# Padding the 64 sample tokens of a streaming encoder layer to full 128-row TensorE tiles

## The chip, the cores and the metric

The kernel runs on one core of a Trainium2 chip. The metric is the time of one execution on the device in microseconds (us); the kernel before was run three times, with a median of 824.62 us (824.10 to 824.93).

## The reference, cut to what matters

One step of a layer with two branches over the same normalised input: an mLSTM (a recurrent matrix memory, worked in chunks) and a latent attention (MLA). 512 prompt tokens start a new stream; 64 sample tokens (`DEC`) continue another one that has 128 cached keys (`PAST`) and a carried mLSTM state. The model width is 1024, with 4 mLSTM heads of 256 and 8 attention heads of 128.

```python
h = rmsnorm(x, norm_g)
(xcm, vm, i_pre, f_pre, o_pre, z_m, c_q, c_kv, k_r, z_a, g_m, g_a) = split_cols(h @ w_in)
# attention, 8 heads; a key chunk of 64 is seen by queries of the same or a later chunk
s = (einsum(qn, kn) + einsum(qr, kr)) * ATT_SCALE
s = where(k_pos // 64 <= q_pos // 64, s, -1e30);  o = softmax(s) @ v
# mLSTM, 4 heads, chunk by chunk: C, n, m are carried
s = (q @ k.T) * w_intra;  num = w_inter * (q @ C) + s @ v;  C = decay * C + (k * w_state).T @ v
y = x + (sig(g_m) * (hm * silu(z_m)) @ w_pm + sig(g_a) * (ha * silu(z_a)) @ w_pa) @ w_out
```

The same weights serve the 512 prompt tokens and the 64 sample tokens.

## The kernel before, in words

Tokens are handled in five tiles (`TILES`, line 34): four of 128 prompt tokens and one of the 64 sample tokens. Keys have six (`KTILES`, line 35): four of the prompt, one of the 128 cached ones, one of the 64 new ones. Most of the arithmetic is done as split products: a float32 operand is cut into a high and a low part (`split_of`, line 103: ScalarE copies the high part, VectorE subtracts) and three matmuls add up.

The large projections are feature-major: `fblock` (line 150) loads a block of 128 weight columns and `gemm_f` (line 121) runs 48 matmuls over all 576 tokens in two halves of 288 columns; line 126 is where all of them are issued. Here the 64 tokens are merely part of the moving columns.

Everything that works token tile by token tile meets the 64 tokens as a tile of its own:

- the first stage: `x_tile` normalises and transposes the input (line 267), `cq_tile` (line 293) and `ck_tile` with `latent` (lines 334 and 335) transpose the latent columns;
- the attention stage: `q_tile` (lines 471 and 472) and `k_tile` (line 502) transpose queries and keys for two heads at a time; `head` (line 524) forms the scores of each prompt tile (lines 529 and 531), adds the chunk mask as a matmul of a one-row operand (line 532: `indrow`, ones for the first 64 queries, times `negrow`, -1e30), and runs `soft` (line 507); the sample tokens' scores are lines 536 and 538, the transposes of their probabilities lines 552 and 553, their product with the values lines 562 and 563;
- the mLSTM stage: `v_block` transposes the values (lines 666 and 670); `mhead` (line 685) goes through the chunks in the order 4, 0, 1, 2, 3, chunk 4 being the 64 sample tokens: scores (line 745), transposed keys (line 758), three-part products through `three` (line 728, called in lines 764, 767 and 771), transposed outputs (line 789).

In each of these the slices `0:L` and `0:DEC` make the operands of the last tile 64 rows, 64 columns, or both. Line 533 is the softmax of a prompt tile:

```python
pe.matmul(ps[:, n - 64:n], indrow, negrow, start=False, stop=True)
pts.append(soft(ps[:, 0:n], P, n))
```

The order of the work: `START` and `PLAN` (lines 31 and 32) are the written order of the steps of the first two stages, and the framework's scheduler then orders each engine's instructions by their data and by a simulated timeline, so that the matmuls of one step stand between those of others. All loads and stores go through SyncE's queue. GpSimd computes the inverse square roots (`rsqrt_of`, line 73) and parts of the rotary embedding.

Of the kernel before, what the change touches and what calls it, by code (L numbers as in the profile page):

```python
# [13 lines left out]
P = 128  # L14
# [3 lines left out]
TK = SEQ + PAST + DEC  # L18
H_M, DH = 4, 256
# [8 lines left out]
# order in which the work of the first two stages is issued (see `steps` and the attention loop)  # L28
# [9 lines left out]
def layer(ctx: ExitStack, tc, A, O):  # L38
# [37 lines left out]
    negrow = const.tile([1, 64], BF16, name="negrow")  # L76
    dve.memset(negrow, NEG)
    indrow = const.tile([1, P], BF16, name="indrow")
    dve.memset(indrow, 0.0)
    dve.memset(indrow[:, 0:64], 1.0)  # L80
# [107 lines left out]
    with ExitStack() as es:  # L188
# [62 lines left out]
        def x_tile(n):  # L251
            t0, L = TILES[n]
            xt = s1.tile([P, D], F32, tag="xt", name="xt", bufs=3)
            sp.dma_start(xt[0:L], A["x_prompt"][t0:t0 + L] if n < 4 else A["x_sample"])
            if n == 0:
                sp.dma_start(nB, A["norm_g"].rearrange("o d -> (o d)").partition_broadcast(P))
            st = s1.tile([P, 8], F32, tag="st", name="st", bufs=3)
            xs = s1.tile([P, D], F32, tag="xs", name="xs", bufs=1)
            act.activation(xs[0:L], xt[0:L], AF.Square, scale=D ** -0.5, accum_out=st[0:L, 0:1])
            dve.tensor_scalar(st[0:L, 1:2], st[0:L, 0:1], EPS, None, ALU.add)  # L260
            rsqrt_of(st[0:L, 2:3], st[0:L, 1:2], L)
            dve.scalar_tensor_tensor(xs[0:L], xt[0:L], st[0:L, 2:3], nB[0:L], ALU.mult, ALU.mult)
            for q in range(2):
                ps = SA()
                for k in range(4):
                    kk = 4 * q + k
                    pe.transpose(ps[:, k * P:k * P + L], xs[0:L, kk * P:(kk + 1) * P], ident[0:L, 0:L])
                pv = ps.rearrange("p (k t) -> p k t", k=4)[:, :, 0:L]
                qk = slice(4 * q, 4 * q + 4)
                split_of(hhi[:, qk, t0:t0 + L], hlo[:, qk, t0:t0 + L], pv)  # L270
                if n == 4:
                    both(hs, qk)

        def cq_tile(n):
# [12 lines left out]
            act.activation(sq[0:L], cq, AF.Square, scale=QL ** -0.5, accum_out=s4[0:L, 0:1])  # L287
            dve.tensor_scalar(s4[0:L, 1:2], s4[0:L, 0:1], EPS, None, ALU.add)
            rsqrt_of(s4[0:L, 1:2], s4[0:L, 1:2], L)
            dve.scalar_tensor_tensor(cqn[0:L], cq, s4[0:L, 1:2], small["qn_g"][0:L], ALU.mult, ALU.mult)  # L290
            ps = SA()
            for k in range(3):
                pe.transpose(ps[:, k * P:k * P + L], cqn[0:L, k * P:(k + 1) * P], ident[0:L, 0:L])
            pv = ps.rearrange("p (k t) -> p k t", k=4)[:, 0:3, 0:L]
            split_of(cqhi[:, :, t0:t0 + L], cqlo[:, :, t0:t0 + L] if n < 4 else cqhi[:, :, T:], pv)
# [35 lines left out]
        def latent(ckn, kro, kt0, L):  # L331
            ps = SA()
            for k in range(2):
                pe.transpose(ps[:, k * P:k * P + L], ckn[0:L, k * P:(k + 1) * P], ident[0:L, 0:L])
            pe.transpose(ps[:, 2 * P:2 * P + L], kro[0:L].rearrange("p a b -> p (a b)"), ident[0:L, 0:L])
# [93 lines left out]
    with ExitStack() as es:  # L429
# [6 lines left out]
        def q_tile(wq, n, qT, qrT):  # L436
# [33 lines left out]
            for hh in range(2):  # L470
                pe.transpose(ps2[:, hh * P:hh * P + L], qs[0:L, hh, 0:NOPE], ident[0:L, 0:L])
                pe.transpose(ps2[:, (2 + hh) * P:(2 + hh) * P + L], q2[0:L, hh].rearrange("p s c -> p (s c)").bitcast(F32), ident[0:L, 0:L])  # L472
# [5 lines left out]
        def k_tile(wk, n, kT, v):  # L478
# [22 lines left out]
            for hh in range(2):  # L501
                pe.transpose(ps2[:, hh * P:hh * P + L], kn[0:L, hh], ident[0:L, 0:L])  # L502
# [4 lines left out]
        def soft(ps, L, n):  # L507
            pt = aq.tile([P, n], F32, tag=f"P{n}", name=f"P{n}", bufs=1)
# [15 lines left out]
        def head(hh, qT, qrT, kT, v, za, ha):  # L524
            pts = []
            for i in range(4):
# [9 lines left out]
            pe.matmul(ps[0:DEC, 0:nk], qT[hh][:, SEQ:T], kT[hh][:, SEQ:TK], start=True, stop=False)  # L536
            for kr in (krhi, krlo):
                pe.matmul(ps[0:DEC, 0:nk], qrT[:, hh, SEQ:T], kr[:, SEQ:TK], start=False, stop=(kr is krlo))
            pt = soft(ps[0:DEC, 0:nk], DEC, nk)
# [12 lines left out]
            pe.transpose(ps[:, 0:DEC], pt[0:DEC, 0:P], ident[0:DEC, 0:DEC])  # L552
            pe.transpose(ps[0:DEC, 64:64 + DEC], pt[0:DEC, P:nk], ident[0:DEC, 0:DEC])
            pTs = aq.tile([P, 2, DEC], F32, tag="pTs", name="pTs", bufs=1)
            act.copy(pTs[:, 0], ps[:, 0:DEC])
            act.copy(pTs[0:DEC, 1], ps[0:DEC, 64:64 + DEC])
# [5 lines left out]
            pe.matmul(ps[:, 128:128 + DEC], v[:, 4, hh], pTs[:, 0], start=True, stop=False)  # L562
            pe.matmul(ps[:, 128:128 + DEC], v[0:DEC, 5, hh], pTs[0:DEC, 1], start=False, stop=True)
            dve.tensor_tensor(za[:, SEQ:T], ps[:, 128:128 + DEC], za[:, SEQ:T], op=ALU.mult)
            split_of(ha[0][:, hh], ha[1][:, hh], za)

        def kq(p):
            qT = [aq.tile([P, T], F32, tag="qT", name="qT", bufs=4) for _ in range(2)]
            qrT = aq.tile([P, 2, T], F32R, tag="qrT", name="qrT", bufs=2)
            kT = [ak.tile([P, TK], F32, tag="kT", name="kT", bufs=4) for _ in range(2)]  # L570
            v = ak.tile([P, 6, 2, VD], F32, tag="v", name="v", bufs=2)
            wk = wload([A["w_ukv"][:, 512 * p:512 * (p + 1)]], 2, 512, cw, 6 * QH)
# [49 lines left out]
    NP = 3 + T + 3  # L622
    DV = DH + 2
    with ExitStack() as es:
# [34 lines left out]
        def v_block(b, va, e):  # L659
            ps = fblock(A["w_in"], O_V + b * P, hx)  # L660
            vf = lp.tile([P, T], F32, tag="vf", name="vf", bufs=1)
# [8 lines left out]
            pe.transpose(ps[0:DEC, 0:P], vf[:, SEQ:T], ident)  # L670
            split_of(va[0][0:DEC, 4, es_], va[1][0:DEC, 4, es_], ps[0:DEC, 0:P])
# [13 lines left out]
        def mhead(h):  # L685
# [17 lines left out]
            qf = lp.tile([P, 2, T], F32, tag="qf", name="qf", bufs=1)  # L703
            kf = lp.tile([P, 2, T], F32, tag="kf", name="kf", bufs=1)
# [7 lines left out]
            # stabilised weights of this head, keys on partitions and queries on the free axis  # L712
# [17 lines left out]
            for c in (4, 0, 1, 2, 3):  # L730
                t0, L = TILES[c]
# [36 lines left out]
                # state  # L768
# [7 lines left out]
                # normalised output  # L776
# [129 lines left out]
```

## Time and profile before

| | |
|---|---|
| median of 3 runs | 824.62 us |
| profiled execution, from first to last instruction (its span) | 822.5 us |
| TensorE matmuls busy | 810.0 us, 98% of the span, 5759 of them |
| VectorE busy | 478.7 us, 58% |
| ScalarE busy | 362.0 us, 44% |
| GpSimd busy | 141.4 us, 17% |
| TensorE clock granted | full in all 40 slices of the span (mean 0.999) |

Of the profiled execution the profile gives the span; its own time is not given beside it, and the median of the runs lies 2.1 us above the span. How to read it: PE is TensorE's matmuls, PEld its weight loads, DVE VectorE, ACT ScalarE, POOL GpSimd. The end of a matmul in the trace is modelled, so a matmul's duration overlaps that of the next one; the starts are what shows the pace. A form such as `64*128 64x64` is rows of the stationary operand * its columns, then rows x columns that stream past it.

### The profile page before, as it was taken

What the parts mean: (1) busy time and instruction counts of PE and PEld (TensorE: products, weight loads), DVE (VectorE), ACT (ScalarE), POOL (GpSimd) and SP (SyncE); (2) the same over time, 40 slices, a digit from 0 to 9 for tenths busy, and PEclk for the clock granted to TensorE, in tenths of its full rate; (3) what the DMA queues carried; (4) which work ended last, traced back from release to release, by engine and by line L of the source; (5) the groups of instructions that cost most, each with busy time, mean ns of one, the idle gap of its engine ahead of it and who ended that gap; (6) DMA issues with size and microseconds to landing.
All of it is one profiled execution on the core that took longest, in us unless ns stands there. A gap on an engine that the chain in (4) does not pass through costs nothing.

```text
span 822.5 us, 14924 instructions
## 1 busy us (share of the span) xinstructions
PE 810.0 (98%) x5759; PEld 761.5 (93%) x5759; DVE 478.7 (58%) x1211; ACT 362.0 (44%) x999; POOL 141.4 (17%) x253
## 2 busy tenths in 40 slices
PE   7899999999999999999999999999999999999998
PEld 6898997888898798889999999999999999999997
DVE  5666566755576658545534873775477355655431
ACT  5446556663555654322434544444454434332200
POOL 2343241410143133001001110110111011000000
PEclk9999999999999999999999999999999999999999
DMA  8431231013113011126223232333333432543332
GB/s 267 138 108 59 74 111 27 1 52 106 41 52 120 27 41 33 46 84 157 78 77 91 66 106 74 103 84 97 91 94 96 118 87 68 165 124 106 101 95 76
DMA packets 101742, 72.80 MB, mean 89 GB/s; under 512 B 5742, under 2 KB 95848, under 8 KB 101672
## 3 DMA queue, kind: packets, MB, share of 16 engines
q1 hardware_dynamic: 101672, 71.86, 30.5%
q8 instruction: 45, 0.74, 0.4%
q14 instruction: 25, 0.20, 0.1%
HBM read 64.24 MB, written 7.61 MB: 87 GB/s over the span
## 4 chain that ended last, share of the span: by engine, by line
PE 94%; DMA 3%; DVE 1%; ACT 1%; issue 0%; SPq 0%; POOL 0%; DVEq 0%; ACTq 0%
PE mm L126 58%; PE sk L143 10%; PE sk L852 3%; PE sa L852 3%; PE sa L529 2%; PE sa L728 2%; PE sa L559 2%; PE sk L728 2%; PE sk L136 2%; PE sa L531 1%; PE sa L547 1%; PE sk L745 1%; PE sa L136 1%; PE sk L502 1%; DMA part<-in_w_in 1%; DMA E<-gscr 1%
## 5 line engine op out<-in xcount | busy, mean ns | idle before, releaser
L105 DVE TENSOR_TENSOR wlo<-raw,whi 128x1024 fp32r<-128x1024 f32 (+1 forms) x88 | 108.5, 1234 | 92.1 <-ACT whi L104 87.1
L104 ACT CAST whi<-raw 128x1024 fp32r<-128x1024 f32 (+1 forms) x88 | 92.6, 1055 | 135.2 <-PE mm L126 91.9
L126 PE MATMUL mm<-hhi,whi 128*128 128x288 f32 x896 | 147.1, 300 | 1.1 <-ACT hhi L104 1.1
L126 PE MATMUL mm<-hhi,wlo 128*128 128x288 f32 x896 | 146.6, 299 | 0.0
L126 PE MATMUL mm<-hlo,whi 128*128 128x288 f32 x896 | 145.7, 298 | 0.0
L126 PEld LDWEIGHTS mm<-hhi,whi 128*128 128x128 f32 x896 | 126.6, 188 | 2.1 <-ACT hhi L104 1.4
L126 PEld LDWEIGHTS mm<-hlo,whi 128*128 128x128 f32 x896 | 127.1, 188 | 1.3 <-issue 0.5
L126 PEld LDWEIGHTS mm<-hhi,wlo 128*128 128x128 f32 x896 | 126.9, 188 | 1.2 <-issue 0.5
L74 POOL TENSOR_TENSOR r<-r,mhalf 128x2 f32<-128x2 f32 (+3 forms) x44 | 37.2, 844 | 165.4 <-DVE r L495 109.4
L126 PE MATMUL mm<-ha,whi 128*128 128x288 f32 x256 | 48.2, 307 | 0.6 <-DVE part L595 0.6
L126 PEld LDWEIGHTS mm<-ha,whi 128*128 128x128 f32 x256 | 37.3, 188 | 2.7 <-DVE part L595 1.1
L511 ACT ACTIVATE P<-sa,sc 128x128 f32<-128x128 f32 (+4 forms) x40 | 20.1, 503 | 36.4 <-DVE sc L510 35.6
L752 POOL TENSOR_TENSOR qi<-qf,wi 128x256 f32<-128x256 f32 (+1 forms) x16 | 11.9, 744 | 105.7 <-ACT qf L710 54.3
L595 DVE TENSOR_TENSOR part<-part,mm 128x288 f32<-128x288 f32 x48 | 21.4, 452 | 11.8 <-PE mm L126 11.6
L74 POOL TENSOR_TENSOR sc<-sc,mhalf 128x1 f32<-128x1 f32 (+1 forms) x20 | 13.0, 648 | 87.0 <-DVE sc L784 87.0
L126 PE MATMUL mm<-ha,wlo 128*128 128x288 f32 x128 | 27.5, 296 | 0.0
L105 POOL TENSOR_TENSOR qi<-qi,qi 128x256 fp32r<-128x256 f32 (+1 forms) x16 | 10.7, 668 | 85.3 <-ACT qi L104 85.3
L529 PE MATMUL sa<-kT,qT 128*128 128x128 f32 (+3 forms) x64 | 23.4, 447 | 0.0
L510 DVE TENSOR_REDUCE sc<-sa 128x1 f32<-128x128 f32 (+4 forms) x40 | 18.3, 457 | 8.5 <-PE sa L532 6.4
L728 PE MATMUL sk<-va,kw 128*128 128x258 f32 (+1 forms) x120 | 22.2, 290 | 0.1
L823 DVE SCALAR_TENSOR_TENSOR mt<-tgm,mm 128x288 f32<-128x288 f32 x16 | 7.3, 454 | 25.1 <-PE mm L126 25.1
L474 ACT ACTIVATE qT<-sk,gqn_c 128x128 f32<-128x128 f32 (+1 forms) x40 | 12.2, 354 | 18.8 <-PE sk L472 18.8
(353 smaller groups left out, 1641.0 us busy)
## 6 DMA issues: line engine op xcount, KB each, us to landing
raw<-in_w_in SPq DMA_DIRECT2D x56, 512.0 KB, 3.8
raw<-in_w_pa SPq DMA_DIRECT2D x8, 512.0 KB
raw<-in_w_pm SPq DMA_DIRECT2D x8, 512.0 KB, 4.2
raw<-in_w_uq SPq DMA_DIRECT2D x4, 576.0 KB, 4.0
gmscr<-tg SPq DMA_DIRECT2D x8, 288.0 KB
tgm<-gmscr SPq DMA_DIRECT2D x8, 288.0 KB, 4.3
xt<-in_x_prompt SPq DMA_DIRECT2D x4, 512.0 KB, 6.7
raw<-in_w_ukv SPq DMA_DIRECT2D x4, 512.0 KB, 3.8
```

Source lines behind the costliest of these rows:

```text
L74: pool.tensor_tensor(dst, ms, mhalf[0:n, 0:dst.shape[-1]], op=ALU.pow)
L104: act.copy(hi, src)
L105: (eng or dve).tensor_tensor(lo, src, hi.bitcast(F32), op=ALU.subtract)
L126: pe.matmul(ps[j], a[:, k0 + k, c0:c0 + P], b[:, k, sl], start=(n == 0), stop=(n == len(trip) - 1))
L136: pe.matmul(out, x[:, k, t0:t0 + P], a, start=(i == 0), stop=(i == len(trip) - 1))
L143: pe.matmul(out, b[:, k, t0:t0 + L], a[:, k, c0:c0 + n], start=(i == 0), stop=(i == len(trip) - 1))
L510: dve.tensor_reduce(sc[0:L, 0:1], ps, AX.X, ALU.max, negate=True)
L511: act.activation(pt[0:L, 0:n], ps, AF.Exp, bias=sc[0:L, 0:1], accum_out=sc[0:L, 1:2])
L529: pe.matmul(ps[:, 0:n], qT[hh][:, q0:q0 + P], kT[hh][:, 0:n], start=True, stop=False)
L595: dve.tensor_tensor(part[:, f, sl], part[:, f, sl], ps[j], op=ALU.add)
L728: pe.matmul(out, x, y, start=(first and i == 0), stop=(last and i == 2))
L852: pe.matmul(ps[0:L, 0:NB], x[:, 4 * u + k, t0:t0 + L], w[u][i][:, k], start=(q == 0), stop=(q == len(trip) - 1))
```

## The change

The last tile's operands become full. Transposes take all 128 rows (what lies in the rows beyond the 64 tokens is not used afterwards). Queries, keys and values of the attention and of the mLSTM get tiles 640 tokens wide (`TP`), whose last 64 columns GpSimd sets to zero; so do the last 64 rows of the values and the last 64 columns of the probabilities (`pt5`). The chunk mask is no longer a matmul: VectorE writes -1e30 into the score tile in PSUM. Two ScalarE copies of the transposed probabilities become one. The merge stage takes other buffers for its gate tiles, and a scratch area for DMA descriptors shrinks, to make room. Comments are dropped.

```diff
+TP = SEQ + P
-    negrow = const.tile([1, 64], BF16, name="negrow")
-    indrow = const.tile([1, P], BF16, name="indrow")
...
-                    pe.transpose(ps[:, k * P:k * P + L], xs[0:L, kk * P:(kk + 1) * P], ident[0:L, 0:L])
+                    pe.transpose(ps[:, k * P:(k + 1) * P], xs[:, kk * P:(kk + 1) * P], ident)
...
-                pe.transpose(ps2[:, hh * P:hh * P + L], qs[0:L, hh, 0:NOPE], ident[0:L, 0:L])
+                pe.transpose(ps2[:, hh * P:(hh + 1) * P], qs[:, hh, 0:NOPE], ident)
...
+        pt5 = aq.tile([P, 2 * P], F32, name="pt5")
+        pool.memset(pt5[:, PAST + DEC:2 * P], 0.0)
...
                 for kr in (krhi, krlo):
-                    pe.matmul(ps[:, 0:n], qrT[:, hh, q0:q0 + P], kr[:, 0:n], start=False, stop=False)
-                pe.matmul(ps[:, n - 64:n], indrow, negrow, start=False, stop=True)
+                    pe.matmul(ps[:, 0:n], qrT[:, hh, q0:q0 + P], kr[:, 0:n], start=False, stop=(kr is krlo))
+                dve.memset(ps[0:DEC, n - DEC:n], NEG)
                 pts.append(soft(ps[:, 0:n], P, n))
...
-            pe.matmul(ps[0:DEC, 0:nk], qT[hh][:, SEQ:T], kT[hh][:, SEQ:TK], start=True, stop=False)
+            pe.matmul(ps[:, 0:nk], qT[hh][:, SEQ:TP], kT[hh][:, SEQ:TK], start=True, stop=False)
...
-            pe.transpose(ps[:, 0:DEC], pt[0:DEC, 0:P], ident[0:DEC, 0:DEC])
-            pe.transpose(ps[0:DEC, 64:64 + DEC], pt[0:DEC, P:nk], ident[0:DEC, 0:DEC])
+            for j in range(2):
+                pe.transpose(ps[:, j * P:(j + 1) * P], pt5[:, j * P:(j + 1) * P], ident)
             pTs = aq.tile([P, 2, DEC], F32, tag="pTs", name="pTs", bufs=1)
-            act.copy(pTs[:, 0], ps[:, 0:DEC])
-            act.copy(pTs[0:DEC, 1], ps[0:DEC, 64:64 + DEC])
+            act.copy(pTs, ps.rearrange("p (k t) -> p k t", k=4)[:, 0:2, 0:DEC])
...
-            pe.matmul(ps[:, 128:128 + DEC], v[0:DEC, 5, hh], pTs[0:DEC, 1], start=False, stop=True)
+            pe.matmul(ps[:, 256:256 + DEC], v[:, 5, hh], pTs[:, 1], start=False, stop=True)
...
-            qT = [aq.tile([P, T], F32, tag="qT", name="qT", bufs=4) for _ in range(2)]
+            qT = [aq.tile([P, TP], F32, tag="qT", name="qT", bufs=4) for _ in range(2)]
+            for hh in range(2):
+                pool.memset(qT[hh][:, T:TP], 0.0)
+            pool.memset(qrT.bitcast(F32)[:, :, T:TP], 0.0)
+            pool.memset(v[DEC:P, 5], 0.0)
...
-            vf = lp.tile([P, T], F32, tag="vf", name="vf", bufs=1)
+            vf = lp.tile([P, TP], F32, tag="vf", name="vf", bufs=1)
+            pool.memset(vf[:, T:TP], 0.0)
...
+            pool.memset(qf[:, :, T:TP], 0.0)
+            pool.memset(kf[:, :, T:TP], 0.0)
...
             for c in (4, 0, 1, 2, 3):
-                t0, L = TILES[c]
+                t0, L = c * P, P
...
-            tg = lp.tile([P, NP], F32, tag=("xp", "th", "vf")[f % 3], name="tgm", bufs=1)[:, 0:T]
+            tg = lp.tile([P, NP if f % 3 == 0 else NP - 3], F32, tag=("xp", "th", "acc")[f % 3], name="tgm", bufs=2 if f % 3 == 2 else 1)[:, 0:T]
...
-    nc = _bacc.Bacc("TRN2", target_bir_lowering=False, num_devices=1)
+    nc = _bacc.Bacc("TRN2", target_bir_lowering=False, num_devices=1, dynamic_dma_scratch_size=1024)
```

The same edit as the first two pairs of lines is made to the transposes of lines 293, 334, 335, 472 and 502, to line 538, and to the value transposes of line 670.

## Rows read from the trace of the kernel before

**Rows 1.** The page's busy table: us, share of the span, instructions of three engines.

```profile
PE 810.0 (98%) x5759; PEld 761.5 (93%) x5759; DVE 478.7 (58%) x1211; ACT 362.0 (44%) x999; POOL 141.4 (17%) x253
```

**Rows 2.** The page's chain of work that ended last, shares of the span.

```profile
PE 94%; DMA 3%; DVE 1%; ACT 1%; issue 0%; SPq 0%; POOL 0%; DVEq 0%; ACTq 0%
```

**Rows 3.** The chain in order of time: start us, us, what; one unbroken run.

```profile
369.05 55.22 PE mm L126 x414
```

**Rows 4.** Timeline of PE around 110 us: start us, us, line, op, tiles, form, count.

```profile
110.08 0.28 PE L531 MATMUL sa<-krhi,qrT 128*128 128x256 f32 x1
110.20 0.28 PE L531 MATMUL sa<-krlo,qrT 128*128 128x256 f32 x1
110.41 0.20 PE L532 MATMUL sa<-negrow,indrow 1*128 1x64 bf16 x1
110.54 1.20 PE L126 MATMUL mm<-hhi,whi 128*128 128x288 f32 x7
111.57 0.83 PE L126 MATMUL mm<-hlo,whi 128*128 128x288 f32 x5
...
112.49 0.65 PE L126 MATMUL mm<-hlo,whi 128*128 128x288 f32 x3
112.97 0.30 PE L126 MATMUL mm<-hhi,wlo 128*128 128x288 f32 x1
```

**Rows 5.** Timeline of PE around 266 us, the query tile of the sample tokens.

```profile
265.69 0.69 PE L126 MATMUL mm<-hlo,whi 128*128 128x288 f32 x4
266.32 0.27 PE L472 MATMUL sk<-ident,q 64*128 64x64 f32 x1
266.43 0.22 PE L471 MATMUL sk<-ident,qs 64*128 64x64 f32 x1
266.49 0.22 PE L472 MATMUL sk<-ident,q 64*128 64x64 f32 x1
266.65 0.80 PE L126 MATMUL mm<-hlo,whi 128*128 128x288 f32 x4
267.29 1.22 PE L126 MATMUL mm<-hhi,wlo 128*128 128x288 f32 x8
```

**Rows 6.** Groups of PE by line and form: xcount | busy us, mean ns.

```profile
L532 PE MATMUL sa<-negrow,indrow 1*128 1x64 bf16 x32 | 6.3, 198 | 0.0
```

**Rows 7.** Timeline of PE around 145 us: the sample tokens' scores lie between these.

```profile
144.88 0.29 PE L126 MATMUL mm<-ha,whi 128*128 128x288 f32 x1
...
145.81 0.32 PE L126 MATMUL mm<-ha,whi 128*128 128x288 f32 x1
```

**Rows 8.** Timeline of PE around 356 us: lines 562 and 563.

```profile
356.23 0.33 PE L562 MATMUL sa<-pTs,v 128*128 128x64 f32 x2
...
356.85 0.40 PE L126 MATMUL mm<-hhi,whi 128*128 128x288 f32 x1
357.09 1.23 PE L126 MATMUL mm<-hlo,whi 128*128 128x288 f32 x8
```

**Rows 9.** Timeline of PE around 438 us: chunk 4's scores and transposed keys.

```profile
437.68 0.42 PE L126 MATMUL mm<-uhi,wlo 128*128 128x288 f32 x2
438.03 0.33 PE L745 MATMUL sk<-qf,kf 128*64 128x64 f32 x2
...
438.35 1.30 PE L126 MATMUL mm<-hhi,whi 128*128 128x288 f32 x8
439.48 0.30 PE L126 MATMUL mm<-hlo,whi 128*128 128x288 f32 x1
```

**Rows 10.** Timeline of PE around 446 us: the 15 products of chunk 4 lie between these.

```profile
445.28 0.29 PE L126 MATMUL mm<-hhi,whi 128*128 128x288 f32 x1
...
447.81 0.71 PE L745 MATMUL sk<-qf,kf 128*128 128x128 f32 x4
```

**Rows 11.** Groups of DVE by line and form: xcount | busy us, mean ns | idle before.

```profile
L195 DVE MEMSET ones<- 128x128 f32 x1 | 0.2, 165 | 0.1
L641 DVE MEMSET xp<- 128x3 f32 x8 | 0.5, 61 | 0.0
```

More of the change, by code (lines that the diff above doesn't have):

```diff
@@ L74, in rsqrt_of @@
         pool.tensor_tensor(dst, ms, mhalf[0:n, 0:dst.shape[-1]], op=ALU.pow)
-    negrow = const.tile([1, 64], BF16, name="negrow")
-    dve.memset(negrow, NEG)
-    indrow = const.tile([1, P], BF16, name="indrow")
-    dve.memset(indrow, 0.0)
-    dve.memset(indrow[:, 0:64], 1.0)
     cols = const.tile([P, 82], F32, name="cols")
@@ L292, in cq_tile @@
             for k in range(3):
-                pe.transpose(ps[:, k * P:k * P + L], cqn[0:L, k * P:(k + 1) * P], ident[0:L, 0:L])
+                pe.transpose(ps[:, k * P:(k + 1) * P], cqn[:, k * P:(k + 1) * P], ident)
             pv = ps.rearrange("p (k t) -> p k t", k=4)[:, 0:3, 0:L]
@@ L333, in latent @@
             for k in range(2):
-                pe.transpose(ps[:, k * P:k * P + L], ckn[0:L, k * P:(k + 1) * P], ident[0:L, 0:L])
-            pe.transpose(ps[:, 2 * P:2 * P + L], kro[0:L].rearrange("p a b -> p (a b)"), ident[0:L, 0:L])
+                pe.transpose(ps[:, k * P:(k + 1) * P], ckn[:, k * P:(k + 1) * P], ident)
+            pe.transpose(ps[:, 2 * P:3 * P], kro.rearrange("p a b -> p (a b)"), ident)
             pv = ps.rearrange("p (k t) -> p k t", k=4)[:, 0:2, 0:L]
@@ L470, in q_tile @@
             for hh in range(2):
-                pe.transpose(ps2[:, hh * P:hh * P + L], qs[0:L, hh, 0:NOPE], ident[0:L, 0:L])
-                pe.transpose(ps2[:, (2 + hh) * P:(2 + hh) * P + L], q2[0:L, hh].rearrange("p s c -> p (s c)").bitcast(F32), ident[0:L, 0:L])
+                pe.transpose(ps2[:, hh * P:(hh + 1) * P], qs[:, hh, 0:NOPE], ident)
+                pe.transpose(ps2[:, (2 + hh) * P:(3 + hh) * P], q2[:, hh].rearrange("p s c -> p (s c)").bitcast(F32), ident)
             for hh in range(2):
@@ L501, in k_tile @@
             for hh in range(2):
-                pe.transpose(ps2[:, hh * P:hh * P + L], kn[0:L, hh], ident[0:L, 0:L])
+                pe.transpose(ps2[:, hh * P:(hh + 1) * P], kn[:, hh], ident)
             for hh in range(2):
@@ L505, in k_tile, with soft @@
             yield
-        def soft(ps, L, n):
-            pt = aq.tile([P, n], F32, tag=f"P{n}", name=f"P{n}", bufs=1)
+        pt5 = aq.tile([P, 2 * P], F32, name="pt5")
+        pool.memset(pt5[:, PAST + DEC:2 * P], 0.0)
+        def soft(ps, L, n, pt=None):
+            pt = aq.tile([P, n], F32, tag=f"P{n}", name=f"P{n}", bufs=1) if pt is None else pt
             sc = ap.tile([P, 4], F32, tag="sc", name="sc", bufs=4)
@@ L535, in head @@
             nk = PAST + DEC
-            pe.matmul(ps[0:DEC, 0:nk], qT[hh][:, SEQ:T], kT[hh][:, SEQ:TK], start=True, stop=False)
+            pe.matmul(ps[:, 0:nk], qT[hh][:, SEQ:TP], kT[hh][:, SEQ:TK], start=True, stop=False)
             for kr in (krhi, krlo):
-                pe.matmul(ps[0:DEC, 0:nk], qrT[:, hh, SEQ:T], kr[:, SEQ:TK], start=False, stop=(kr is krlo))
-            pt = soft(ps[0:DEC, 0:nk], DEC, nk)
+                pe.matmul(ps[:, 0:nk], qrT[:, hh, SEQ:TP], kr[:, SEQ:TK], start=False, stop=(kr is krlo))
+            soft(ps[:, 0:nk], P, nk, pt5[:, 0:nk])
             pT = aq.tile([P, 10 * P], F32, tag="pT", name="pT", bufs=1)
@@ L561, in head @@
             dve.tensor_tensor(za[:, 0:SEQ], of, za[:, 0:SEQ], op=ALU.mult)
-            pe.matmul(ps[:, 128:128 + DEC], v[:, 4, hh], pTs[:, 0], start=True, stop=False)
-            pe.matmul(ps[:, 128:128 + DEC], v[0:DEC, 5, hh], pTs[0:DEC, 1], start=False, stop=True)
-            dve.tensor_tensor(za[:, SEQ:T], ps[:, 128:128 + DEC], za[:, SEQ:T], op=ALU.mult)
+            pe.matmul(ps[:, 256:256 + DEC], v[:, 4, hh], pTs[:, 0], start=True, stop=False)
+            pe.matmul(ps[:, 256:256 + DEC], v[:, 5, hh], pTs[:, 1], start=False, stop=True)
+            dve.tensor_tensor(za[:, SEQ:T], ps[:, 256:256 + DEC], za[:, SEQ:T], op=ALU.mult)
             split_of(ha[0][:, hh], ha[1][:, hh], za)
         def kq(p):
-            qT = [aq.tile([P, T], F32, tag="qT", name="qT", bufs=4) for _ in range(2)]
-            qrT = aq.tile([P, 2, T], F32R, tag="qrT", name="qrT", bufs=2)
+            qT = [aq.tile([P, TP], F32, tag="qT", name="qT", bufs=4) for _ in range(2)]
+            qrT = aq.tile([P, 2, TP], F32R, tag="qrT", name="qrT", bufs=2)
+            for hh in range(2):
+                pool.memset(qT[hh][:, T:TP], 0.0)
+            pool.memset(qrT.bitcast(F32)[:, :, T:TP], 0.0)
             kT = [ak.tile([P, TK], F32, tag="kT", name="kT", bufs=4) for _ in range(2)]
             v = ak.tile([P, 6, 2, VD], F32, tag="v", name="v", bufs=2)
+            pool.memset(v[DEC:P, 5], 0.0)
             wk = wload([A["w_ukv"][:, 512 * p:512 * (p + 1)]], 2, 512, cw, 6 * QH)
@@ L669, in v_block @@
             ps = SK()
-            pe.transpose(ps[0:DEC, 0:P], vf[:, SEQ:T], ident)
-            split_of(va[0][0:DEC, 4, es_], va[1][0:DEC, 4, es_], ps[0:DEC, 0:P])
+            pe.transpose(ps[:, 0:P], vf[:, SEQ:TP], ident)
+            split_of(va[0][:, 4, es_], va[1][:, 4, es_], ps[:, 0:P])
         def gate_block(b, gate, e):
@@ L702, in mhead @@
             w = wload([A["wq_m"][h], A["wk_m"][h]], 4, DH)
-            qf = lp.tile([P, 2, T], F32, tag="qf", name="qf", bufs=1)
-            kf = lp.tile([P, 2, T], F32, tag="kf", name="kf", bufs=1)
+            qf = lp.tile([P, 2, TP], F32, tag="qf", name="qf", bufs=1)
+            kf = lp.tile([P, 2, TP], F32, tag="kf", name="kf", bufs=1)
+            pool.memset(qf[:, :, T:TP], 0.0)
+            pool.memset(kf[:, :, T:TP], 0.0)
             for dst, k0, s in ((qf, 0, 0.5), (kf, 2, 0.5 / 16.0)):
@@ L789, in mhead @@
                     pe.transpose(ps[:, e * P:e * P + L], hn[0:L, e * P:(e + 1) * P], ident[0:L, 0:L])
-                dve.tensor_tensor(tm[:, :, t0:t0 + L], ps.rearrange("p (k t) -> p k t", k=4)[:, 0:2, 0:L],
-                                  gate[:, :, t0:t0 + L], op=ALU.mult)
+                n = TILES[c][1]
+                dve.tensor_tensor(tm[:, :, t0:t0 + n], ps.rearrange("p (k t) -> p k t", k=4)[:, 0:2, 0:n],
+                                  gate[:, :, t0:t0 + n], op=ALU.mult)
             for s, dst in ((0, Cp), (1, Cs)):
```

## The prediction

> **What bounds the kernel now.** I read the busy table first: TensorE's matmuls fill 98% of the span, VectorE 58%, ScalarE 44%, GpSimd 17% [rows 1]. A busy share alone proves nothing, so the chain of waits came next: 94% of the work that ended last is PE's, 3% DMA, 1% each VectorE and ScalarE [rows 2]. So the time is PE's instruction stream, and an edit is worth what it takes out of that stream. Matmul durations overlap, so I price by start times. The pace of the large projections is the yardstick: 414 matmuls in 55.22 us, or 0.1334 us each [rows 3]. Wherever the timeline shows k of them between two starts, I take k x 0.1334 off, and what is left is the price of what stands among them.
>
> **What a small operand costs.** The query tile of the sample tokens shows it [rows 5]: from 265.69 to 267.29 are 1.60 us with eight projection matmuls (1.067), so three 64-row transposes cost 0.533. Three full transposes of a prompt tile, between 111.57 and 112.97 [rows 4], cost 1.40 - 1.067 = 0.333, 0.11 each. Yet inside the small group the last two start only 0.06 apart (266.43, 266.49) [rows 5]: at 0.06 each the three would be 0.18. The other 0.35 is paid on going into the small form and coming out of it. A group of k small transposes thus loses 0.35 in the change of form, and padding adds 0.05 to each: a group of one gains 0.30, of two 0.25, of three 0.20, of eight loses 0.05.
>
> **The sum, part by part.**
>
> *The mask matmul* (line 532, 32 times [rows 6]). From 110.20 to 111.57 are 1.37 us: one L531 at 0.12 (110.08 to 110.20), seven projections (0.934), and 0.316 for the mask, almost all of it form change [rows 4]. 32 x 0.316 = 10.1 us, the largest term. The sizes other than this one (256 columns) are taken alike.
>
> *The transposes.* Query tiles: four in each of four pairs of heads; [rows 5] has three together and the fourth elsewhere, so 0.20 + 0.30, four times: 2.0. Key tiles: two each, four times, together (0.25) or apart (0.60); I take 0.42, halfway, as both occur: 1.7. Probabilities (lines 552, 553): a pair for each of eight heads: 2.0. Outputs of chunk 4 (line 789): four pairs, 1.0. First stage: a group of eight (-0.05), one of three (0.20), latents as two and one (0.25 + 0.30): 0.7. Together 7.4; were every group kept whole, 4 x 0.35 and 4 x 0.17 less, 5.3. The transposes of line 670 have 128 rows already, 64 columns only; the trace has no row that splits off their cost. I take nothing, nearest to the full transposes; the other end is eight pairs' worth less padding, 2 us.
>
> *Scores of the sample tokens* (lines 536, 538). From 144.88 to 145.81 are 0.93, less one projection, 0.80 [rows 7]. Padded, the float32 ones have 192 columns: from 0.11 for 128 [rows 4], 0.165 each, two. The other two lie between 0.06 [rows 5] and the 0.12 of a 256-column L531 [rows 4]; I take 0.09, as columns scale. That is 0.51, so 0.29 a head, 2.3 in all (0.23 to 0.35: 1.8 to 2.8).
>
> *Products with the values* (lines 562, 563). From 356.23 to 357.09, less one projection, are 0.727 [rows 8]. Four full ones cost between 4 x 0.06 and 4 x 0.11; I take the upper, because their stationary operand is that of a full transpose. 0.29 a head, 2.3 (up to 3.9).
>
> *mLSTM chunk 4.* Scores and a key transpose: 437.68 to 439.48 less ten projections is 0.466 [rows 9]; three full ones 0.33; 0.13, eight times: 1.1. The 15 products: 445.28 to 447.81 less one projection is 2.40 [rows 10]; at 258 of 288 columns a full one is 0.12, 15 are 1.80; 0.60, four times: 2.4.
>
> Sum: 10.1 + 7.4 + 2.3 + 2.3 + 1.1 + 2.4 = 25.6 us.
>
> **What is added.** 32 memsets on VectorE, each 64 x 64 in PSUM. The nearest rows are 0.061 for three columns and 0.165 for 128, both in SBUF [rows 11]; I take 0.12, 3.8 us on an engine with 42% free. On the softmax's path they replace a matmul that took 0.316, so that path does not grow even at 0.165. Their wait is not new: the row maximum behind them on VectorE already waits for the same scores. Some 33 memsets on GpSimd (four for each pair of heads, one for each value block, two for each mLSTM head, one once) zero 64 columns; its price for that is not in my rows. GpSimd is busy 17% [rows 1], so I cost them at nothing; cover gone, they hold up the inverse square roots queued behind them, which key and query tiles wait for. ScalarE loses one copy a head; VectorE, ScalarE and GpSimd work on 64 more columns in chunk 4. All of it lies beside PE's stream. SyncE's queue is untouched: no transfer is added or moved. The scratch size and the other buffers for the gate tiles are taken at nothing: neither adds an instruction to PE's stream.
>
> **What comes back.** The savings are thickest in the attention stage. PE then arrives earlier at places where it has just caught up with VectorE or GpSimd, and the scheduler may lay the stream out anew. Between nothing and half of the gain can be lost there. I take 1.0 us, near the lower end, because VectorE and ScalarE together hold 2% of the chain [rows 2].
>
> Net 24.6 us off the profiled span of 822.5: 797.9. The median of the runs is 2.1 above that span, which I keep: 800.0, equally 824.62 - 24.6.
>
> **The rivals.**
>
> *Half of it turns into waits.* Softmax and key chains set the pace where PE no longer does: 824.6 - 12.8 = 811.8. For it: VectorE rises to some 482 of 798 us. Against it: the chain of waits [rows 2], and that the chain through the mask gets shorter. Chance 0.15.
>
> *Only the padding is paid (slower).* The 0.35 could be no price of the form but of meeting an operand that another engine has just written; it would then stay behind the padded forms, and the change would add 0.05 to 62 transposes and to 16 scores of chunk 4, 3.9 us, and take away only the masks' own column time, 32 x 0.06 = 1.9: +2.0, 826.6. It decides if a padded group still costs 0.35 above its members. Against it stands the full triple [rows 4], whose operands come from the same engines and which shows no such extra. The Trainium skill, in TensorEngine Tiling (Array Packing), section Theoretical Speedup, speaks for this rival: an operand of at most 64 rows or columns is there worth up to twice the pace, so padding would give that away. The trace agrees inside a group (0.06 against 0.11), not for a group as a whole. Chance 0.06.
>
> *More than the sum.* The value products at 0.06 give 1.6 more, line 670 up to 2, the narrower masks some more, and nothing comes back: 824.6 - 25.6 - 3.9 = 795.1. Chance 0.06.
>
> *It does not do what it says.* A new order of the stream that costs as much as is saved, or forms that stay small in the built program: 824.6. Chance 0.03.
>
> **How the numbers follow.** The forecast has 0.70: 800.0, the time of the likeliest case, from about 797 to 804 by the bounds of its terms. The range 794 to 812 takes in the case above the sum and, at its edge, the half-lost one; beyond it lie the two last rivals and the far part of the half-lost one, under 2 in 10. Faster by over 0.2% (1.65 us, about what a measurement of this kernel can tell from no change) are the forecast, the half-lost and the larger gain, 0.91; within it the idle change, 0.03; slower the padding rival, 0.06.
>
> **What would show it.** PE's matmul count falls by 32, to 5727, and of the forms with 64 rows or 64 columns at the lines named none is left. L531's successors start at the ordinary pace; a query triple of the sample tokens costs 0.33 instead of 0.53; chunk 4's 15 products take about 1.8 instead of 2.4 us. The large projections stay at 0.1334 us and the clock stays full. Each is a step of the sum. The forecast is wrong if a padded group still pays 0.35 (the padding rival), or if the forms are gone, the groups are cheap and the PE timeline shows new idle time before transposes of probabilities (line 547), keys (502) or queries (471), released by VectorE or GpSimd: then the half-lost rival holds, and the sum was right but not the cover.

## The result, and the profile after

| | before | after |
|---|---|---|
| median of the runs, us | 824.36 (823.66 to 824.93, 4 runs) | 809.76 (808.73 to 810.22, 4 runs) |
| ratio to before | | 0.9816, 95% interval 0.9803 to 0.9829 |
| profiled execution: span, us | 822.5 | 808.4 |
| PE matmuls | 5759 | 5727 |

The change gains 14.6 us. The forecast was 24.6 (800.0), so its sign and its range hold, but the time lies nearer to the half-lost rival (811.8) than to the forecast. Some 10 us of the forecast gain did not come.

The busy table of the page after, and below it the chain that ended last:

```profile
PE 791.6 (98%) x5727; PEld 762.3 (94%) x5727; DVE 481.0 (60%) x1240; ACT 362.2 (45%) x991; POOL 148.2 (18%) x286
...
PE 91%; DVE 4%; DMA 3%; ACT 1%; issue 1%; SPq 0%; POOL 0%; ACTq 0%; POOLq 0%
```

PE's share is 98% again, as in [rows 1], and shows nothing of the loss. The chain does: VectorE's share goes from 1% to 4%, PE's from 94% to 91% [rows 2].

**Prices of the sum, looked up.** The timeline of PE, first where the mask was, then a query tile of the sample tokens, then chunk 4 of the mLSTM (start us, us, line, operation, tiles, form, count). Line numbers have moved: 530 was 531, 467 and 468 were 471 and 472, 733 was 728.

```profile
109.03 0.28 PE L530 MATMUL sa<-krlo,qrT 128*128 128x256 f32 x1
109.14 0.29 PE L122 MATMUL mm<-hhi,wlo 128*128 128x288 f32 x1
...
232.01 0.43 PE L122 MATMUL mm<-ha,wlo 128*128 128x288 f32 x2
232.28 0.27 PE L468 MATMUL sk<-ident,q 128*128 128x128 f32 x1
232.39 0.27 PE L467 MATMUL sk<-ident,qs 128*128 128x128 f32 x1
232.50 0.27 PE L468 MATMUL sk<-ident,q 128*128 128x128 f32 x1
232.52 0.78 PE L122 MATMUL mm<-ha,whi 128*128 128x288 f32 x4
233.14 0.42 PE L122 MATMUL mm<-ha,wlo 128*128 128x288 f32 x2
...
436.04 0.41 PE L733 MATMUL sk<-va,kw 128*128 128x258 f32 x2
...
437.86 0.61 PE L750 MATMUL sk<-qf,kf 128*128 128x128 f32 x4
```

- Behind the second L530 (109.03) the next projection starts 0.11 later, at the ordinary pace, and nothing stands between them.
- From 232.01 to 233.14 are 1.13 us with six projections (0.80): the padded triple costs 0.33, as forecast. With 64 rows it was 0.53 [rows 5].
- The 15 products of chunk 4 take 1.82 us (436.04 to 437.86), forecast 1.80; before it was 2.40 [rows 10].
- The sample tokens' products with the values take 0.39 where a head of the middle has them unhindered (lines 560 and 561, from 151.82 to 152.21), forecast 0.44; before it was 0.73 [rows 8].

**The added work.** The memset of the mask on VectorE (count | busy, mean ns | idle before):

```profile
L531 DVE MEMSET sa<- 64x64 f32 x32 | 3.5, 112 | 7.0 <-PE sa L530 6.6
```

It took 0.112 us where 0.12 was the estimate. The 33 memsets that zero columns or rows are on GpSimd. Its busy time grows by 6.8 us (141.4 to 148.2), and in the list of waits below PE never waits for it.

**Where the gain comes through and where not.** The chain in order of time has one landmark in both kernels, the unbroken run of 414 projections behind the attention stage; it stood at 369.05 [rows 3]:

```profile
360.14 55.22 PE mm L122 x414
```

Up to this run 8.9 us are gained (369.05 - 360.14). The forecast's terms for that part (masks 10.1, scores 2.3, value products 2.3, and of the transposes all but chunk 4's outputs, 6.4) add up to 21.1. Behind it 5.2 are gained (822.5 - 369.05 = 453.5, against 808.4 - 360.14 = 448.3), forecast 4.5 (1.1, 2.4 and 1.0). So the mLSTM terms were about right, and 12 us of loss lie ahead of this run, where the attention stage is. PE's waits from 100 us to that run, the wait at its start included (engine, line, waited for: us in total, times, longest), first before, then after:

```profile
PE mm L126 <- DVE part L595: 0.6, 2, 0.4
```

```profile
PE mm L122 <- ACT ha L100: 1.2, 1, 1.2
PE mm L122 <- DVE part L597: 0.8, 3, 0.4
PE sk L139 <- DVE qs L439: 0.5, 1, 0.5
PE sa L546 <- ACT pT L547: 0.5, 1, 0.5
PE sa L528 <- ACT qT L470: 0.5, 1, 0.5
PE sa L530 <- DVE qrT L471: 0.4, 1, 0.4
PE sa L546 <- ACT P L510: 0.2, 1, 0.2
PE sk L132 <- DVE qrT L471: 0.2, 1, 0.2
PE sk L498 <- DVE kn L494: 0.2, 1, 0.2
PE sk L498 <- ACT kT L500: 0.2, 1, 0.2
```

One row becomes ten, 0.6 us becomes 4.7: beside part, the running sum of the output projections, PE now waits for query tiles (qs, qT, qrT), key tiles (kn, kT), probabilities (P, pT) and the last head's output (ha). The prediction had named waits of this kind as the sign of the half-lost rival. Between 160 and 300 us the list has no wait of PE at all.

The largest sit at the last head. The timeline of its end, PE and what it waits for:

```profile
342.47 1.26 PE L546 MATMUL sa<-ident,P 128*128 128x128 f32 x7 [0.22 <-ACT P L510]
...
344.20 0.33 PE L546 MATMUL sa<-ident,P 128*128 128x128 f32 x1 [0.46 <-ACT pT L547]
...
347.06 0.39 PE L561 MATMUL sa<-pTs,v 128*128 128x64 f32 x2
347.10 0.69 DVE L559 TENSOR_TENSOR za<-sa,za 128x512 f32<-128x512 f32 x1 [2.52 <-PE sa L557]
347.70 0.21 DVE L562 TENSOR_TENSOR za<-sa,za 128x64 f32<-128x64 f32 x1
347.95 0.67 ACT L100 CAST ha<-za 128x576 fp32r<-128x576 f32 x1 [2.90 <-DVE za L562]
348.67 1.20 PE L122 MATMUL mm<-ha,whi 128*128 128x288 f32 x5 [1.22 <-ACT ha L100]
```

No projection stands among the transposes of the probabilities here, so each chain is seen at its full length: exponential, transpose, copy, transpose; and at the end value product, VectorE's two products, ScalarE's cast, next projection. In the kernel before the last head's instructions lie among the 96 projections of the gate blocks G6 and G7 (48 each) and PE is never idle, as the windows of the kernel before show (us; busy us of PE, PEld, DVE, ACT, POOL with counts; granted clock; DMA share; GB/s):

```profile
340.00:350.00 10.00, 10.00 (x70) 8.67 (x69) 5.04 (x14) 4.07 (x10) 0.70 (x2) 1.00 0.16 52
350.00:360.00 10.00, 10.00 (x66) 8.82 (x66) 3.00 (x5) 3.15 (x8) 0.00 (x0) 1.00 0.29 84
```

In the kernel after the scheduler has placed G6 and G7 ahead of the last head, though the written plan is the same, and nothing is left to put beside it. Why it did so is not shown.

The windows of the end of this stretch, after:

```profile
346.00:349.00 3.00, 1.78 (x12) 1.46 (x11) 1.17 (x3) 0.67 (x1) 0.00 (x0) 1.00 0.00 0
349.00:354.00 5.00, 4.85 (x24) 4.39 (x23) 1.74 (x5) 0.00 (x0) 0.00 (x0) 0.67 0.01 3
```

PE is busy 1.78 of 3 us, and in the 5 us behind that the granted clock is 0.67 on average, between the full level of 2.4 GHz and 1.2 GHz: some 1.65 us (0.33 x 5) in this execution.

### The profile page after: what moved, and what is told of

It reads as the page before. It is cut to its first block, busy times and chain, and to the rows that moved or that the text cites. A ratio compares the mean times of both kernels' runs of the same rounds, so it can differ in the third digit from the quotient of the medians.

```text
span 808.4 us, 14939 instructions
## 1 busy us (share of the span) xinstructions
PE 791.6 (98%) x5727; PEld 762.3 (94%) x5727; DVE 481.0 (60%) x1240; ACT 362.2 (45%) x991; POOL 148.2 (18%) x286
## 4 chain that ended last, share of the span: by engine, by line
PE 91%; DVE 4%; DMA 3%; ACT 1%; issue 1%; SPq 0%; POOL 0%; ACTq 0%; POOLq 0%
PE mm L122 58%; PE sk L139 9%; PE sa L858 3%; PE sk L858 3%; PE sa L733 2%; PE sa L557 2%; PE sk L733 2%; PE sk L132 2%; PE sa L528 2%; PE sk L750 1%; PE sa L546 1%; PE sa L132 1%; PE sa L530 1%; DMA part<-in_w_in 1%; PE sk L498 1%; DMA E<-gscr 1%
## 5 line engine op out<-in xcount | busy, mean ns | idle before, releaser
L122 PE MATMUL mm<-ha,whi 128*128 128x288 f32 x256 | 50.3, 314 | 2.0 <-ACT ha L100 1.2
L122 PEld LDWEIGHTS mm<-ha,whi 128*128 128x128 f32 x256 | 39.0, 194 | 5.4 <-DVE part L597 2.2
L75 POOL TENSOR_TENSOR sc<-sc,mhalf 128x1 f32<-128x1 f32 x20 | 12.1, 605 | 84.9 <-DVE sc L789 84.9
L101 POOL TENSOR_TENSOR qi<-qi,qi 128x256 fp32r<-128x256 f32 x16 | 11.8, 737 | 71.6 <-ACT qi L100 71.6
L510 ACT ACTIVATE P<-sa,sc 128x128 f32<-128x128 f32 (+3 forms) x32 | 16.9, 527 | 16.7 <-DVE sc L509 16.5
L733 PE MATMUL sk<-va,kw 128*128 128x258 f32 x120 | 21.5, 284 | 0.1
L122 PEld LDWEIGHTS mm<-ha,wlo 128*128 128x128 f32 x128 | 21.0, 192 | 0.0
```

Of the source, the lines that this page charges most:

```text
L75: pool.tensor_tensor(dst, ms, mhalf[0:n, 0:dst.shape[-1]], op=ALU.pow)
L101: (eng or dve).tensor_tensor(lo, src, hi.bitcast(F32), op=ALU.subtract)
L122: pe.matmul(ps[j], a[:, k0 + k, c0:c0 + P], b[:, k, sl], start=(n == 0), stop=(n == len(trip) - 1))
L510: act.activation(pt[0:L, 0:n], ps, AF.Exp, bias=sc[0:L, 0:1], accum_out=sc[0:L, 1:2])
L733: pe.matmul(out, x, y, start=(first and i == 0), stop=(last and i == 2))
```

## The experiments

Three theories stood against each other, by the names that the expectations use. **Form**: what was lost or won lies in the operands' forms themselves. **Order**, later called **fill** or **cover**: the chains of the heads, the last one's above all, are no longer beside enough projections, and the place of the plan's blocks decides. **Pace**: VectorE's and ScalarE's chains set the pace of the whole attention stage, however the projections lie. All ratios are to the kernel before, run on the same chip; its medians there were 824.36 to 825.19 us. The variants change the form or the order of the work, not its result.

| kernel | median us | ratio [95% interval] |
|---|---|---|
| mask alone | 817.96 | 0.9911 [0.9895, 0.9928] |
| mLSTM padding alone | 819.96 | 0.9936 [0.9921, 0.9950] |
| after, one-row mask matmul kept | 818.11 | 0.9915 [0.9900, 0.9930] |
| after, mask matmul with 128 rows | 812.80 | 0.9848 [0.9831, 0.9864] |
| after | 809.76 | 0.9816 [0.9803, 0.9829] |
| after, G7 held | 809.51 | 0.9810 [0.9795, 0.9825] |
| after, G6 and G7 held | 808.87 | 0.9802 [0.9787, 0.9817] |
| after, G5 late | 807.53 | 0.9793 [0.9777, 0.9810] |
| after, G5 late, G6 and G7 held | 807.94 | 0.9796 [0.9783, 0.9809] |
| after, G4 and G5 late | 808.59 | 0.9803 [0.9789, 0.9816] |
| before, G5 late | 826.29 | 1.0017 [1.0008, 1.0026] |
| before, G6 and G7 early | 828.84 | 1.0045 [1.0029, 1.0062] |

### Is it the form of the mask, or the mask?

Two kernels from the one after, each with the mask as a matmul again. In the first its operands have one row, as before. In the second the same matmul has 128 rows, 127 of them zero:

```diff
-                    pe.matmul(ps[:, 0:n], qrT[:, hh, q0:q0 + P], kr[:, 0:n], start=False, stop=(kr is krlo))
-                dve.memset(ps[0:DEC, n - DEC:n], NEG)
+                    pe.matmul(ps[:, 0:n], qrT[:, hh, q0:q0 + P], kr[:, 0:n], start=False, stop=False)
+                pe.matmul(ps[:, n - 64:n], indrow, negrow, start=False, stop=True)
...
-    negrow = const.tile([1, 64], BF16, name="negrow")
+    negrow = const.tile([P, 64], BF16, name="negrow")
+    dve.memset(negrow, 0.0)
+    dve.memset(negrow[0:1], NEG)
```

(indrow likewise.) Expected of the one-row mask:

> The changed kernel with the chunk mask put back as the one-row matmul, everything else padded. Form theory (a change of operand form costs PE about 0.16 us on the way in and again on the way out, and PE is the pace): 32 masks at 0.32 us come back, 809.8 + 10 = 820, between 816 and 821. Pace theory (other engines set the pace of the attention stage now, PE has slack there): the masks are mostly hidden, 810 to 814.

Expected of the full one:

> As the run before, but the mask's two operands are filled with zeros to 128 rows: the same 32 matmuls in the same places of PE's stream, no change of form. Form theory: each costs its own 0.03 to 0.11 us instead of 0.32, so 7 to 9 us below the run with the one-row mask, 811 to 813. If the price were that of the instruction or of its wait: the same time as the run with the one-row mask.

Measured 818.11 and 812.80, each inside the form theory's range: 5.3 us by the form of the operands alone, less than the 7 to 9 expected between the two. The same place in both timelines, the one-row mask first:

```profile
108.91 0.28 PE L535 MATMUL sa<-krlo,qrT 128*128 128x256 f32 x1
109.12 0.20 PE L536 MATMUL sa<-negrow,indrow 1*128 1x64 bf16 x1
109.25 0.33 PE L473 MATMUL sk<-ident,q 128*128 128x128 f32 x1
...
109.55 0.38 PE L127 MATMUL mm<-hhi,wlo 128*128 128x288 f32 x1
```

```profile
107.95 0.28 PE L536 MATMUL sa<-krlo,qrT 128*128 128x256 f32 x1
108.08 0.20 PE L537 MATMUL sa<-negrow,indrow 128*128 128x64 bf16 x1
108.11 0.31 PE L474 MATMUL sk<-ident,q 128*128 128x128 f32 x1
...
108.40 0.38 PE L128 MATMUL mm<-hhi,wlo 128*128 128x288 f32 x1
```

From the score matmul to the next projection, with the same three transposes between, are 0.64 us with the one-row mask and 0.45 with the full one. So the change of form costs 0.19 here, 32 times 6.1, of which 5.3 reach the end. The kernel after has no mask matmul but a projection more in this bracket (109.03 to 109.52, 0.49 - 0.133 = 0.36). So the one-row mask costs 0.28 in this place (0.32 in [rows 4]), and 0.09 of that is the matmul itself. The forecast had put "almost all of it" down to the form; the total, which is what the sum used, was right.

### Which part of the change pays?

The mask alone in the kernel before (the memset in place of the matmul, no padding), and the mLSTM stage alone padded:

```diff
-                pe.matmul(ps[:, n - 64:n], indrow, negrow, start=False, stop=True)
+                dve.memset(ps[0:DEC, n - DEC:n], NEG)
```

> The kernel before with the chunk mask alone replaced by the VectorE memset; all 64-row forms stay. Form theory: 10 us less PE stream in the attention stage, of which some turns into waits where the stage's fill runs out: 7 to 10 us faster than before, 815 to 818. Pace theory: the softmax chains take over at once, 3 to 5 us faster, 820 to 822.

```diff
-            qf = lp.tile([P, 2, T], F32, tag="qf", name="qf", bufs=1)
+            qf = lp.tile([P, 2, TP], F32, tag="qf", name="qf", bufs=1)
+            pool.memset(qf[:, :, T:TP], 0.0)
...
-                t0, L = TILES[c]
+                t0, L = c * P, P
```

> The kernel before with the mLSTM stage alone padded (value transposes, chunk 4, the merge's buffers). In that stage PE is covered by projections everywhere, so every change of form that goes is gained. Form theory: the sum of its terms, 1.1 + 2.4 + 1.0 = 4.5 us faster than before, between 4 and 5.5 (820 against 825). A theory in which half of any saving turns into waits: 2.2 us.

The mask alone gains 7.0 us of its 10.1, at the lower end of what was expected. PE's wait for the last head's ha (1.1 us) is there already with nothing padded. The mLSTM part gains 5.0, a little over its 4.5. The padding without the mask's edit gains 7.1 (the kernel with the one-row mask), and taking off the mLSTM's 5.0 leaves some 2 for all that was padded ahead of it, priced at 11.0. So most of what was priced for the padding of the attention stage was lost, and the mLSTM term was not.

### Does the last head lack its cover?

Three kernels put projections beside the last head, by an edit of the order alone. In the plan H6 and H7 are the heads of the last pair, P3 is their output projection, and G0 to G7 are the gate blocks. In the first two kernels G7, or G6 and G7, can't be issued until the third score tile of the last head is computed; in the third the plan has G5 behind the last pair's heads. The edit of the second (the first has 7 alone), and that of the third:

```diff
-                gm_block(i, aq.tile([P, T], F32, tag="tg", name="tg", bufs=1))
+                with tc.issue_after(gate_ins[0]) if i in (6, 7) else ExitStack():
+                    gm_block(i, aq.tile([P, T], F32, tag="tg", name="tg", bufs=1))
```

> The changed kernel, only the gate block G7 (48 projection matmuls) is held behind the third score tile of the last attention head, so that it again lies among that head's softmax and transposes. Order theory (the scheduler put G6 and G7 ahead of the last head, whose 5 us of waits are now bare): 3 to 5 us faster than the changed kernel, 805 to 807. Pace theory: the waits only move, 809 to 811.

> As the run before, with G6 held back as well: the last head is covered as in the kernel before, but the head before it is left without projections. Order theory: the last head gains 5 us and the head before it loses 1 to 4, 806 to 809, above the run that holds G7 alone. Pace theory: 809 to 811.

```diff
-PLAN = "... H4 G4 Z5 Z6 H5 G5 K3 Z7 P2 H6 H7 G6 G7 P3"
+PLAN = "... H4 G4 Z5 Z6 H5 K3 Z7 P2 H6 H7 G5 G6 G7 P3"
```

> The changed kernel with one token of the written order moved: gate block G5 (48 projections, 6.4 us) goes from before key block K3 to the last three fill blocks, so that both last heads have projections to lie among. Fill theory (the last heads' chains are longer than the PE work now left to cover them, 6 to 7 us of waits; the middle has work to spare): 4 to 6 us faster than the changed kernel, 804 to 806. If the stage as a whole is bound by other engines, the waits turn up in the middle instead: 808 to 811.

G7 held gave 809.51, nothing gained, as the pace theory had it and outside the order theory's 805 to 807. G6 and G7 held gave 808.87, 0.9 less than after: inside the order theory's 806 to 809, though not above the kernel that holds G7 alone, and not told from nothing, as the intervals overlap. PE's waits in the second from 310 to 333 us say why (its lines stand up to three further on than after's):

```profile
PE sa L538 <- ACT qT L470: 0.9, 1, 0.9
PE sa L555 <- DVE pt L512: 0.7, 1, 0.7
PE sa L549 <- ACT pT L550: 0.6, 1, 0.6
PE sa L531 <- DVE qrT L471: 0.4, 1, 0.4
PE sk L468 <- DVE q L463: 0.4, 1, 0.4
```

The last head is covered now, as the window of this kernel shows:

```profile
340.00:350.00 10.00, 10.00 (x69) 9.10 (x68) 3.63 (x5) 2.82 (x6) 0.00 (x0) 1.00 0.28 82
```

The head before it, from which the two blocks were taken, waits instead, 3.0 us in these rows.

G5 late gave 807.53, the lowest of all and 2.2 under after: short of the 804 to 806 expected, and under the 808 to 811 of the rival, though the intervals of the two ratios still overlap (0.9777 to 0.9810, and 0.9803 to 0.9829). Its windows show PE full where it was bare, and the wait for ha at the end still there:

```profile
340.00:346.00 6.00, 6.00 (x41) 5.21 (x40) 2.25 (x3) 2.17 (x5) 0.00 (x0) 1.00 0.16 55
346.00:349.00 3.00, 1.78 (x12) 1.41 (x12) 1.58 (x3) 0.67 (x1) 0.00 (x0) 1.00 0.59 167
349.00:354.00 5.00, 4.85 (x36) 4.62 (x35) 2.72 (x7) 0.00 (x0) 0.00 (x0) 1.00 0.02 3
```

The clock stays full behind that wait, where the kernel after had lost some 1.65 us. So much of the gain in the profiled execution is the clock's: the run of 414 starts at 357.56 in place of 360.14, 2.6 earlier, and 1.65 of that is the clock. Among the runs whose mean granted clock is 1.000, G5 late took 807.12 and 807.35 and the kernel after 808.73, which puts the order's own share at some 1.5 us. And waits turn up where G5 was taken away: from 285 to 335 us PE now waits three times for part, 1.1 us in total, where the kernel after has 0.2 (and 0.4 for qrT).

The same edit in the kernel before, as a control:

> The same move of G5 in the kernel before. Fill theory: there the last heads were covered already, so nothing is gained, within 1.5 us of before, 823.5 to 826.5. If the move helped by itself, whatever the forms, it would gain as much here as in the padded kernel, 4 us or more.

It gave 826.29, 1.3 us slower and inside the 823.5 to 826.5 expected: where the last head has its cover, the move brings nothing.

### The same loss without any padded form

The plainest test of the theory: the kernel before, all small forms and masks kept, and only the order of the plan edited so that G6 and G7 come ahead of the last pair's heads.

```diff
-PLAN = "... K3 Z7 P2 H6 H7 G6 G7 P3"
+PLAN = "... K3 Z7 P2 G6 G7 H6 H7 P3"
```

> The kernel before, small forms and mask matmuls kept, with the blocks G6 and G7 of the plan put ahead of the last pair's score pass, so that the last head's softmax, transposes and value products have no projection matmuls beside them. Cover theory (what the change lost in the attention stage is the projections that used to cover each head's chain, above all the last head's): the bare last head costs 4 to 6 us in this kernel too, 828.5 to 831 us, with new PE waits on VectorE and ScalarE in the last 20 us of the attention stage. Theory that the loss comes with the padded forms or the memset: no padded form is here, 823.5 to 826 us.

828.84, 3.7 us slower than before on the same chip (825.15) and inside the cover theory's numbers. The four runs spread: the two with a mean granted clock of 1.000 took 826.75 and 827.84, the two with 0.998 took 829.83 and 829.95. Its waits at the last head are those of the kernel after, line for line (ACT ha, ACT pT, ACT P):

```profile
PE mm L126 <- ACT ha L104: 1.1, 1, 1.1
PE sa L547 <- ACT pT L548: 0.5, 1, 0.5
PE sa L547 <- ACT P L511: 0.2, 1, 0.2
```

And so is the clock behind them (its windows):

```profile
356.00:363.00 7.00, 5.45 (x25) 3.42 (x25) 3.56 (x9) 2.02 (x7) 0.00 (x0) 1.00 0.22 65
363.00:368.00 5.00, 4.85 (x24) 4.58 (x23) 1.76 (x4) 0.00 (x0) 0.00 (x0) 0.66 0.00 0
```

The run of 414 starts at 373.69 in its chain, 4.6 us later than before [rows 3], of which 1.7 is that clock (0.34 x 5). So the bare last head alone costs some 3 us here, 1.6 and 2.7 in the two runs at the full clock.

### Can all of it be covered by the order?

Two more orders of the kernel after: G5 late together with G6 and G7 held, and G4 and G5 both moved behind a score pass.

```diff
-PLAN = "... H4 G4 Z5 Z6 H5 G5 K3 Z7 P2 H6 H7 G6 G7 P3"
+PLAN = "... H4 Z5 Z6 H5 G4 K3 Z7 P2 H6 H7 G5 G6 G7 P3"
```

> The kernel after, with G5 moved behind the last score pass and G6 and G7 held until the last head's third score tile. Cover theory with a fixed supply of projections: the last head is covered, but what covers it is missing in the two heads ahead of it, so 806 to 808 us, no better than G5 alone moved (807.5) by more than 1.5. If the last head alone were the loss (and the heads ahead had cover to spare): its bare tail, some 5 us of the 6.7 over the pace there, comes back as well, 803 to 805 us.

> The kernel after, with G4 moved behind the third pair's score pass and G5 behind the last pair's, so that every late head has a block beside it. Cover theory: 805 to 807.5 us, as G5 alone moved gave 807.5 and some of the cover of heads 2 to 4 is not needed (little excess over the pace between 200 and 300 us). Theory that VectorE's and ScalarE's chains set the pace of the whole stage however the projections lie: 808 to 811 us.

807.94 and 808.59. The first is inside the cover theory's numbers and outside the other's: to cover the last head better no longer helps. The second misses the cover theory's 805 to 807.5 and lies in the pace theory's 808 to 811. There the bare end is back, at 345 to 355 us, with the wait for ha (1.2 us) and a granted clock of 0.83, and it was not followed further. No order tried came below 807.5; whether one can is open.

## Why the prediction was right or wrong

**Right: the bound and the sign.** PE's stream set the time, and taking small forms out of it made it shorter. The rival by which padding only costs (826.6) falls with the triple of 0.33: the price sits in the form and goes with it. What the Trainium skill states in TensorEngine Tiling (Array Packing), section Theoretical Speedup, up to twice the pace for operands of at most 64 rows or columns, does not show here as far as it spoke for that rival: these padded groups cost less, 0.33 against 0.53.

**Right: the terms, where they can be looked up.** The mask's 0.32 is gone in every place; the triple, the 15 products (1.82 for 1.80), the value products (0.39 for 0.44) and the mLSTM stage (5.0 alone, 5.2 in the kernel after, for 4.5) came about as priced. The prices of the key tiles, the probabilities, the scores and the first stage were not looked up one by one, but together they can be: with each form at the pace that it keeps in the kernel after and the masks at nothing, PE's starts from 100 us to the run of 414 are 20.3 us over in the kernel before, 0.6 of it waits. The terms there were priced at 20.4 (21.1 less the first stage's 0.7). In the kernel after they are still 11.7 over, with no small form left. So the prices were about right in sum, and what is lost are waits and the clock. That "almost all" of the mask's price was the form was wrong (0.19 of 0.32), without effect on the sum, since the mask went as a whole.

**Right: what is added.** 0.112 us for VectorE's memset, GpSimd's hidden.

**Luck: the range.** It holds by its edge. The bounds of the terms alone gave 797 to 804, and 812 was set to take in the half-lost rival; that 809.76 lies inside is owed to that width and not to the sum.

**Wrong: "What comes back."** This is the step that failed: "I take 1.0 us, near the lower end, because VectorE and ScalarE together hold 2% of the chain [rows 2]". Some 11 us came back where 1.0 was put down (25.6 by the sum, 14.6 measured). The 2% was read as a reserve. It only says that these chains were seldom last while projections lay beside them. A head's chain through softmax, transposes, copies and value products has a length of its own, which the edit hardly touches; what shrank was PE's work beside it, and what changed was the order in which the scheduler lays that work. The kernel before with G6 and G7 early shows how little the 2% protects: the same two engines, no padding, and 3.7 us lost, the clock's part included.

Where it went in the profiled execution, by PE's starts against the pace that each form keeps elsewhere in the stream (0.1334 us for 288 columns, 0.11 for a transpose):

- The last head: from 339.48 to 348.67 are 9.2 us, and its instructions need about 5.1 (two L530 0.5, two projections 0.3, four sample scores 0.5, twelve transposes 1.3, eight value products 2.15, four small ones 0.4). 4.1 lost, and 1.65 more by the clock behind it, which the prediction had as staying full.
- Key and query tiles between 140 and 160 us, where the first pair's last head runs: 2.4, with PE's waits for qs, qT, qrT and kn in it.
- Query tiles of the last pair around 312: 1.4, with the wait for qrT.

These make 9.6 of the 12 us that are lacking. For the first item the experiments show the cause: taking the cover away costs it in the kernel before, and putting it back removes the bare stretch, but then waits turn up where the cover came from, so that no more than about 2 us were won back. For the two others only the waits are shown. Most of the rest is scattered in pieces of under 1 us, by the same count: 0.4 between 120 and 140 us, 0.7 between 200 and 220, and 0.9 between 350 and 360 beside the clock's part.

**The half-lost rival**, at 0.15, came nearest, and its signs came in part. PE waits at transposes of probabilities and keys; for queries it waits at the score matmuls (lines 528 and 530) and at query projections (lines 139 and 132), not at the transposes. The waits are for VectorE as named, but for ScalarE too, and none is for GpSimd. Its mechanism, chains that set the pace, holds in the three places above and not over the whole stage: from 160 to 300 us the list has no wait of PE, and its starts are 0.8 us over pace in all.

## What to carry to other kernels

A chain's small share of the critical path is no reserve: before an edit shortens the bounding engine's stream, count in each stage what lies beside every chain, and ask what is left of it when the stream is shorter and laid anew. Price a cut only where enough other work remains to fill in; here the mLSTM stage gave all of its term, and what lies ahead of it gave 8.9 of 21.1 us. In this kernel a one-row operand among full ones cost 0.19 us more than the same matmul with 128 rows, and three transposes of 64 rows cost 0.20 more than three full ones; such lone small matmuls were worth padding or moving to another engine.

## What was not expected of the hardware

- The clock behind a bare stretch. After PE's waits at the last head the granted clock was 0.67 and 0.66 over 5 us in the kernel after and in the one before with G6 and G7 early, while with the last head covered (before, 350 to 360) it was 1.00. It does not always fall: the kernel with G5 late has the same bare stretch (PE busy 1.78 us of 3) and kept 1.00 over the 5 us behind it, and the kernel with the one-row mask has a last head as bare (PE busy 2.44 and 2.78 us of two stretches of 4) and kept 1.00 too. Of the four runs of the kernel after, the one with a mean granted clock of 1.000 took 808.73, the three with 0.997 to 0.999 took 809.73 to 810.22. The mean does not tell where it fell: in the profiled execution of G5 late (0.998) it was 0.66 from 10 to 15 us. What decides it was not settled.
- A one-row mask's change of form costs 0.19 us, about what the padding gave back on a whole triple of 64 rows (0.53 - 0.33 = 0.20), and a full matmul of only 64 columns cost about 0.1 (0.45 - 0.36), near a full transpose (0.11).
